# Rotation tables times the norm factor, level exponents by sign of scale, and a gating norm folded past its product

## The chip, the cores and the metric

The kernel runs on one core of a Trainium2 chip. The metric is device time in microseconds (us), the median of three runs. The core has TensorE (PE, matrix products, with its weight loads as PEld), VectorE (DVE), ScalarE (ACT) and GpSimd (POOL), and the queue of SyncE (SP), which here only issues DMA transfers. TensorE's clock has two levels, 1.2 and 2.4 GHz; the granted clock in the tables is its mean share of the upper one.

## The reference

A token matrix x of 512 by 1024 goes through two layers of a first block and one layer of a second block, all in float32.

- **First block, per layer.** h = rmsnorm(x) and one wide projection h @ w_in, whose columns feed three mixers. The *NSA mixer* has rotary positions on its queries and keys, a compressed branch over pooled key blocks, and two causal softmax branches, each weighted by a gate. The *GLA mixer* is a gated linear attention over chunks of 64 tokens; with b the running sum of log gates, pair (i, j) of a chunk is weighted by exp((b_i - b_j)/16). *Spatial gating* takes gelu(uv), splits it into u and v, puts v through a layernorm with gain g and bias b, mixes its tokens within chunks of 128 by a lower triangular matrix per group, adds a bias, and multiplies by u. The three results are concatenated, projected by w_out and added to x; a SwiGLU feed-forward layer follows.
- **Second block.** A gated linear recurrence in both directions beside a neighbourhood attention, two merge gates, an output projection w_o that is scaled and added to x1 = rmsnorm(x) * final_norm, and a last rmsnorm.

## The kernel before

Activations lie as eight tiles of 128 features by 512 tokens. Each float32 operand of a large product is split into a high and a low part, and each product is three matmuls of 512 columns (`three`). A weight chunk of 128 x 1024 comes by a DMA from the SP queue into `raw`; ScalarE rounds it to `whi` (L90, in `halves`) and `wlo` = raw - whi is one subtraction (L93). `turn` decides which engine does that subtraction: from L369, at the start of a layer's mixers, to L887, at their end, every second one goes to GpSimd, and otherwise all go to VectorE.

The mixers of a layer are nine generators, and the string WEAVE gives the order in which their steps are issued (WEAVE2 does the same in the second block). A scheduler then orders the instructions of each engine by its own time model; every engine runs its list in order and waits on semaphores. All tiles of 128 x 512 share 74 buffers (`slot`), and PSUM has eight banks.

The steps that matter here:

- `rotary`: a projection p is multiplied by the broadcast norm factor `rb` (L674, VectorE), and the result q1 is copied with its 32-row blocks exchanged into q2 by four DMAs from GpSimd's queue (L677). One projection later `finish` forms q1 times cosine (L648, VectorE), q2 times sine (L649, GpSimd) and their sum (L650, VectorE), and splits it into a query or a key (L659 and L660, or L663 to L667).
- `level` of `gla`: six levels per layer. GpSimd subtracts a reference column from each half of the running sum b with opposite signs (L465, L466), ScalarE takes one exponential (L467), and VectorE multiplies by k and q (L470, L471). The small products of 32 x 32 (`gram`) read the result.
- `gating`: the normalised v is multiplied by a gain and increased by a bias on GpSimd (L707, L708) before it enters the token mixing product.
- `compressed`: the softmax rows are scaled by a broadcast factor on GpSimd (L759).
- In the second block GpSimd multiplies x by its norm factor `rb1` (L1197), ScalarE multiplies by the gain (L1198) and the result is stored to HBM in `xdram` (L1199). It is loaded again before the last projection (L1224).

Of the kernel before, what the change touches and what calls it, by code (L numbers as in the profile page):

```python
# [16 lines left out]
P = 128  # L17
# [20 lines left out]
def body(tc, a, out):  # L38
# [37 lines left out]
        return slice(t * P, (t + 1) * P)  # L76


    turn = [0, 0]

    def fetch(src, n):
        raw = wraw.tile([P, 1024], F32, tag="raw", name="raw")
        dma(raw[:, :n], src)
# [2 lines left out]
    def halves(raw, nk, width):  # L86

        n = nk * width
        hi = whl.tile([P, 1024], F32R, tag="whi", name="whi")
        A.activation(hi[:, :n], raw[:, :n], AF.Copy)  # L90
        lo = whl.tile([P, 1024], F32R, tag="wlo", name="wlo")
        turn[0] += 1
        (G if turn[1] and turn[0] % turn[1] == 0 else V).tensor_tensor(lo[:, :n], raw[:, :n], hi[:, :n].bitcast(F32), op=ALU.subtract)  # L93
        return (hi[:, :n].rearrange("p (k c) -> p k c", c=width),
                lo[:, :n].rearrange("p (k c) -> p k c", c=width))

# [237 lines left out]
    for l in range(LAYERS):  # L334
# [31 lines left out]
        first = gemm(wi[6], act, lambda: stat.append(rsqrt(tok_stat(acc, D)[:], NT)))  # L366
        rs = stat[0]
        rb = bcast(rs)
        turn[1] = 2  # L369
        dma(gw[:16, :128], a["gla_w_up"][l])  # L370
        dma(gw[:, 128:132], a["gla_cols"][l])
        sv = [slot(shape=(P, 2, 256)) for _ in range(2)]
# [33 lines left out]
        def gla():  # L406
# [52 lines left out]
            def level(s_):  # L459
                n = S // (2 * s_)  # L460
                bb = b.rearrange("p (n h s) -> p n h s", h=2, s=s_)
                ref = bb[:, :, 0, s_ - 1:s_].to_broadcast([P, n, s_])
                X = slot()
                Xv = X.rearrange("p (n h s) -> p n h s", h=2, s=s_)
                G.tensor_tensor(Xv[:, :, 0], ref, bb[:, :, 0], op=ALU.subtract)  # L465
                G.tensor_tensor(Xv[:, :, 1], bb[:, :, 1], ref, op=ALU.subtract)  # L466
                A.activation(X[:], X[:], AF.Exp, scale=1.0 / 16)  # L467
                qv = q_.rearrange("p (n h s) -> p n h s", h=2, s=s_)
                kv = k_.rearrange("p (n h s) -> p n h s", h=2, s=s_)
                V.tensor_tensor(Xv[:, :, 0], Xv[:, :, 0], kv[:, :, 0], op=ALU.mult)  # L470
                V.tensor_tensor(Xv[:, :, 1], Xv[:, :, 1], qv[:, :, 1], op=ALU.mult)  # L471
                return X
# [169 lines left out]
        def rotary():  # L642
            for e in range(2):
                dma(trig[e][:], a["c_trig"][:, e])
            dma(amask[:], a["c_amask"])
            def finish(i, q1, q2):
                qr = slot()
                V.tensor_tensor(qr[:], q1[:], trig[0][:], op=ALU.mult)  # L648
                G.tensor_tensor(q2[:], q2[:], trig[1][:], op=ALU.mult)  # L649
                V.tensor_tensor(qr[:], qr[:], q2[:], op=ALU.add)  # L650
                if i < 4:
                    qn[i] = qr
                for g in range(2):
                    o = half[1 - g]
                    s_ = half[g]
                    t_ = slot(F32R)
                    if i < 4:
                        qs[4 * g + i] = t_
                        A.activation(t_[s_], qr[s_], AF.Copy, scale=0.125)  # L659
                        V.scalar_tensor_tensor(t_[o], qr[s_], 0.125, t_[s_].bitcast(F32), op0=ALU.mult, op1=ALU.subtract)  # L660
                    else:
                        kd[2 * (i - 4) + g] = t_
                        A.activation(t_[s_], qr[s_], AF.Copy)  # L663
                        A.activation(t_[o], qr[s_], AF.Copy)
                        l_ = slot(F32R)
                        G.memset(l_[o].bitcast(F32), 0.0)
                        V.tensor_tensor(l_[s_], qr[s_], t_[s_].bitcast(F32), op=ALU.subtract)  # L667
                        kl[2 * (i - 4) + g] = l_

            prev = None  # L670
            for i in (4, 5, 0, 1, 2, 3):
                p = proj(i)
                q1 = slot()
                V.tensor_tensor(q1[:], p[:], rb[:], op=ALU.mult)  # L674
                q2 = slot()
                for b_ in range(4):
                    dmag(q2[32 * b_:32 * b_ + 32], q1[32 * (b_ ^ 1):32 * (b_ ^ 1) + 32])  # L677
                if prev:
                    finish(*prev)
                prev = (i, q1, q2)  # L680
                yield
            finish(*prev)
            yield


        def gating():
            gb2 = slot(shape=(P, 2, 256))
            dma(gb2[:], a["sg_gb"][l].partition_broadcast(P))
            wT = slot(shape=(P, 4, P))
            dma(wT[:], a["sg_wT"][l])  # L690
            G.affine_select(wT[:], wT[:], pattern=[[0, 4], [1, P]], compare_op=ALU.is_ge, fill=0.0, base=0, channel_multiplier=-1)
            for g in range(4):
                dma(bs[half[g % 2], g // 2], a["sg_b"][l, g].partition_broadcast(64))
            mv = small.tile([P, NT, 2], F32, tag="sgmv", name="sgmv")
            for th in range(2):
                gelu2(sv[th].rearrange("p a b -> p (a b)"), sv[th].rearrange("p a b -> p (a b)"), S, slot(), slot())
# [7 lines left out]
            for t in range(NT):  # L704
                vg = sv[t // 2][:, t % 2]
                V.tensor_scalar(vg, vg, mv[:, t, 0:1], rl[:, t:t + 1], op0=ALU.subtract, op1=ALU.mult)
                G.tensor_tensor(vg, vg, gb2[:, 0], op=ALU.mult)  # L707
                G.tensor_tensor(vg, vg, gb2[:, 1], op=ALU.add)  # L708
            us = []
            for gp_ in range(2):  # L710
                p = proj(12 + gp_)
# [5 lines left out]
            for gp_ in range(2):  # L717
                u = us[gp_]
                p = bank()
                for t in range(NT):  # L720
                    for par in range(2):
                        g = 2 * gp_ + par
                        mm(p[half[par], tsl(t)], sv[t // 2][:, t % 2, 64 * g:64 * g + 64], wT[:, g])
                s1 = slot()
                V.tensor_tensor(s1.rearrange("p (t i) -> p t i", t=NT), p.rearrange("p (t i) -> p t i", t=NT),
                                bs[:, gp_, None, :].to_broadcast([P, NT, P]), op=ALU.add)
                V.tensor_tensor(s1[:], s1[:], u[:], op=ALU.mult)
                split(s1[:], osg[gp_][0][:], osg[gp_][1][:], 0.5)
            yield
# [4 lines left out]
        def compressed():  # L734
            dma(cm[:], a["c_cmask"])
            pcs = []
            for ih in range(2):
# [18 lines left out]
                for i in range(2):  # L756
                    sv_ = sm.rearrange("p (q i g) -> p q i g", q=NT, i=2)[:, :, i]
                    V.tensor_tensor(sv_, sv_, gate[:, :, 6 * ih + 3 * i::12], op=ALU.mult)
                G.tensor_tensor(pcf, pcf, sm[:, :, None].to_broadcast([P, 16, 32]), op=ALU.mult)  # L759
                pcs.append(pc)  # L760
            yield
            for ih in range(2):
# [121 lines left out]
            for _ in t:  # L884
                pass

        turn[1] = 0  # L887

        heads = ogla + osg + onsa
        x = [slot() for _ in range(KT)]  # L890
# [301 lines left out]
    for n, c in enumerate(WEAVE2):  # L1192
# [1 line left out]
        if n == 0:  # L1194
            rb1 = bcast(rsqrt(tok_stat(acc, D)[:], NT))
        if n < KT:
            G.tensor_tensor(x[n][:], x[n][:], rb1[:], op=ALU.mult)  # L1197
            A.activation(x[n][:], x[n][:], AF.Copy, scale=norms[:, 4, n:n + 1])  # L1198
            dma(xdram[:, n], x[n][:])  # L1199
    for c in "rpn":  # L1200
        for _ in tasks[c]:
# [20 lines left out]
    xo = [slot() for _ in range(KT)]  # L1222
    for j in range(KT):
        dma(xo[j][:], xdram[:, j])  # L1224
    for j in range(KT - 1):
        p = gemm(a["w_o"][j], mg)
        V.scalar_tensor_tensor(xo[j][:], p[:], mod[:, 2, j:j + 1], xo[j][:], op0=ALU.mult, op1=ALU.add)
# [89 lines left out]
def _prep(inp):  # L1317
# [32 lines left out]
    gn = np.concatenate([inp["gla_norm"]] * 2, 1)  # L1350
    z = np.zeros_like(gn)
    r["gla_cols"] = np.ascontiguousarray(np.stack([inp["gla_b_up"], gn, z, z], 2))
    r["sg_gb"] = np.stack([inp["sg_ln_g"], inp["sg_ln_b"]], 1)
    r["sg_wT"] = np.ascontiguousarray(inp["sg_w"].transpose(0, 3, 1, 2))
    r["sg_b"] = inp["sg_b"]
    rows = np.concatenate([np.concatenate([np.arange(64 * i, 64 * i + 64), np.arange(64 * (i + 4), 64 * (i + 4) + 64)])
# [57 lines left out]
```

## Time and profile before

| | |
|---|---|
| median of 3 runs | 1908.09 us (1907.3 to 1911.67) |
| the profiled execution | 1909.09 us, span 1907.4 us |
| mean granted TensorE clock | 0.986 |
| busy, share of the span | PE 97%, DVE 58%, ACT 43%, POOL 15% |
| first layer's mixers | about 30 to 251 us |
| second layer's mixers | about 690 to 907 us |
| second block | about 1319 us to the end |

A stretch is read from the span's start. Busy time of TensorE counts pipelined matmuls, which overlap, so a busy TensorE is not yet one at full rate: a 512-column matmul follows the one before after about 0.22 us at the upper clock level and after about 0.43 us at the lower. A wait names the instruction that released the waiting one.

### The profile page before, as it was taken

How to read it: one execution, taken by the hardware profiler on the slowest of the kernel's cores; microseconds unless marked ns; L12 is line 12 of the kernel's file. 1: busy time of each engine (PE TensorE's matmuls, PEld its weight loads, DVE VectorE, ACT ScalarE, POOL GpSimd, SP SyncE). 2: the span in 40 equal slices, each digit the busy share in tenths (PEclk: the TensorE clock that was granted, in tenths of full speed). 3: DMA queues.
4: the chain of work that ended last, by engine and by line, in shares of the span. 5: the costliest groups of instructions: out<-in, count | busy, mean ns of one | idle time of the engine just before them, and what ended most of it. 6: DMA issues, size and time to landing. Idle time of an engine off the chain costs nothing.

```text
span 1907.4 us, 27296 instructions
## 1 busy us (share of the span) xinstructions
PE 1853.2 (97%) x10770; PEld 1510.4 (79%) x10770; DVE 1100.0 (58%) x2043; ACT 822.8 (43%) x1406; POOL 280.9 (15%) x346
## 2 busy tenths in 40 slices
PE   8899999999999998999999999999989999999997
PEld 7677678888888886876788888888778878888886
DVE  5778754756642346978445555324568867664333
ACT  6345732323222233456323322223477857662223
POOL 3643011000000035620200000011600030000003
PEclk9999999999999998999999999999999999999998
DMA  8421032544533372310332332332433342322331
GB/s 249 147 79 56 1 107 90 186 144 132 166 109 117 106 235 64 99 34 1 131 96 93 100 100 90 98 93 84 138 116 97 103 135 88 100 89 89 99 133 67
DMA packets 71441, 203.22 MB, mean 107 GB/s; under 512 B 11632, under 2 KB 15120, under 8 KB 71312
## 3 DMA queue, kind: packets, MB, share of 16 engines
q1 hardware_dynamic: 66768, 192.03, 31.5%
q0 software_dynamic: 4544, 9.44, 2.0%
q8 instruction: 84, 1.38, 0.3%
q14 instruction: 45, 0.37, 0.1%
HBM read 186.23 MB, written 6.29 MB: 101 GB/s over the span
## 4 chain that ended last, share of the span: by engine, by line
PE 91%; DVE 4%; ACT 2%; issue 1%; DMA 1%; POOL 0%; SPq 0%; POOLq 0%; DVEq 0%; ACTq 0%
PE bank L45 88%; PE bank L806 2%; PE bank L1122 1%; ACT whi L90 1%; DVE wlo L93 1%; DVE b L789 0%; DVE b L660 0%; DMA raw<-w_in_m 0%; DVE b L470 0%; DVE b L648 0%; ACT b L267 0%; ACT b L1037 0%; DMA raw<-w_gate 0%; DMA c<-c 0%; ACT b L1105 0%
## 5 line engine op out<-in xcount | busy, mean ns | idle before, releaser
L45 PE MATMUL bank<-b,whi 128*128 128x512 f32 (+1 forms) x4220 | 1299.5, 390 | 0.0
L45 PEld LDWEIGHTS bank<-b,whi 128*128 128x128 f32 x4220 | 788.9, 189 | 164.8 <-issue 5.1
L45 PE MATMUL bank<-b,wlo 128*128 128x512 f32 (+1 forms) x2110 | 818.7, 388 | 0.2 <-DVE wlo L93 0.2
L90 ACT ACTIVATE whi<-raw 128x1024 fp32r<-128x1024 f32 (+2 forms) x290 | 298.8, 1032 | 713.4 <-PE bank L45 465.0
L93 DVE TENSOR_TENSOR wlo<-raw,whi 128x1024 fp32r<-128x1024 f32 (+3 forms) x273 | 330.4, 1211 | 296.6 <-ACT whi L90 291.7
L45 PEld LDWEIGHTS bank<-b,wlo 128*128 128x128 f32 x2110 | 398.6, 189 | 83.6 <-issue 1.6
L45 PE MATMUL bank<-b 32*32 32x32 f32 (+9 forms) x2956 | 201.0, 260 | 18.5 <-DVE b L471 8.2
L217 POOL TENSOR_TENSOR b<-b 128x512 f32<-128x512 f32 x33 | 50.8, 1546 | 1001.4 <-ACT b L211 1001.2
L45 PEld LDWEIGHTS bank<-b 32*32 32x32 f32 (+3 forms) x2956 | 134.1, 128 | 71.0 <-issue 49.0
L45 PE MATMUL bank<-whi,b 128*128 128x512 f32 (+1 forms) x384 | 111.5, 370 | 6.8 <-ACT b L267 6.8
L272 ACT ACTIVATE b<-b 128x512 fp32r<-128x512 f32 x76 | 48.0, 632 | 136.5 <-DVE b L926 92.2
L792 ACT ACTIVATE b<-b,nm 128x384 f32<-128x384 f32 (+3 forms) x128 | 71.0, 559 | 34.6 <-DVE nm L789 34.2
L45 PEld LDWEIGHTS bank<-whi,b 128*128 128x128 f32 x384 | 71.3, 195 | 16.9 <-ACT b L267 6.8
L789 DVE CUSTOM_DVE_ANT_0 b<-bank,b 128x384 f32<-128x384 f32 (+3 forms) x128 | 56.8, 485 | 26.5 <-PE bank L45 26.5
L45 PE MATMUL bank<-wlo,b 128*128 128x512 f32 (+1 forms) x192 | 70.2, 368 | 0.0
L924 DVE TENSOR_TENSOR b<-bank,b 128x512 f32<-128x512 f32 x44 | 30.3, 689 | 65.1 <-PE bank L45 65.1
L922 DVE TENSOR_TENSOR b<-bank,b 128x512 f32<-128x512 f32 x44 | 30.3, 688 | 52.7 <-PE bank L45 51.9
L274 DVE TENSOR_TENSOR b<-b 128x512 fp32r<-128x512 f32 x72 | 49.7, 691 | 18.6 <-ACT b L272 18.6
L324 DVE SCALAR_TENSOR_TENSOR b<-raw,silc,b 128x512 f32<-128x512 f32 x42 | 29.6, 747 | 36.6 <-DMA raw<-w_c 36.6
L806 PEld LDWEIGHTS bank<-c_ident,b 128*128 128x128 f32 x320 | 35.5, 141 | 18.8 <-DVE b L796 5.7
L806 PE MATMUL bank<-c_ident,b 128*128 128x128 f32 x320 | 46.8, 278 | 3.7 <-DVE b L796 3.7
L93 POOL TENSOR_TENSOR wlo<-raw,whi 128x1024 fp32r<-128x1024 f32 x17 | 41.3, 2427 | 51.7 <-ACT whi L90 49.9
(254 smaller groups left out, 1511.6 us busy)
## 6 DMA issues: line engine op xcount, KB each, us to landing
raw<-w_in SPq DMA_DIRECT2D x56, 512.0 KB, 3.5
raw<-w_gate SPq DMA_DIRECT2D x44, 512.0 KB, 3.5
raw<-w_up SPq DMA_DIRECT2D x44, 512.0 KB, 3.5
raw<-w_down SPq DMA_DIRECT2D x32, 512.0 KB, 3.5
raw<-w_in_t SPq DMA_DIRECT2D x28, 512.0 KB, 3.8
raw<-w_c SPq DMA_DIRECT2D x24, 512.0 KB, 3.5
b<-cmp_w SPq DMA_DIRECT2D x32, 256.0 KB, 7.4
raw<-w_out SPq DMA_DIRECT2D x16, 512.0 KB, 3.5
```

Source lines behind the costliest of these rows:

```text
L45: T.matmul(o, l, r, start=st, stop=sp)
L90: A.activation(hi[:, :n], raw[:, :n], AF.Copy)
L93: (G if turn[1] and turn[0] % turn[1] == 0 else V).tensor_tensor(lo[:, :n], raw[:, :n], hi[:, :n].bitcast(F32), op=ALU.subtract)
L217: self.eng.tensor_tensor(self.acc[:], self.acc[:], self.last[:], op=ALU.add)
L272: A.activation(hi, src, AF.Copy, scale=scale)
L274: V.tensor_tensor(lo, src, hi.bitcast(F32), op=ALU.subtract)
L324: V.scalar_tensor_tensor(ma[e][:], r_, sc_[:, k:k + 1], ma[e][:], op0=ALU.mult, op1=ALU.add)
L789: V.tensor_tensor_reduce(out=pg[qb], in0=p, in1=amask[:, S - w:], op0=ALU.add, op1=ALU.min, scale=-1.0, scalar=-NEG, accum_out=nm[:, qb:qb ...
L792: A.activation(pg[qb], pg[qb], AF.Exp, bias=nm[:, qb:qb + 1], scale=-1.0, accum_out=dn[:, qb:qb + 1])
L806: T.transpose(p[:, c0 + (qb - kb) * P:c0 + (qb - kb + 1) * P], ph[g][qb][:, tsl(kb)], ident[:])
L922: V.tensor_tensor(g1[:], pg[:], rb[:], op=ALU.mult)
L924: V.tensor_tensor(u1[:], pu[:], rb[:], op=ALU.mult)
```

## The change

It takes the two-input elementwise operations of 128 x 256 and larger off GpSimd in the mixers and in the second block's start, and changes some of the arithmetic around them. All splits of weights go to VectorE. A level becomes one subtraction b - ref over the whole tile on VectorE, and two exponentials on half tiles with scales -1/16 and +1/16. The cosine and sine tables are multiplied by `rb` once per layer on VectorE; the projection is copied to q1 by ScalarE unscaled, the cosine product reads the projection's bank, and the sine product moves to VectorE. The gating gain is applied behind the token mixing product, and its bias is folded into the additive term through the column sums of the triangular matrix (four small products with a vector of ones per layer, two small VectorE operations). The spill of x is stored as it is, and norm factor and gain are applied on VectorE after it is loaded again; `rb1` is kept until then. GpSimd keeps its memsets, copies, DMA issues, the triangular select, the small powers, and the sums of squares (L217).

```diff
     def halves(raw, nk, width):
...
-        turn[0] += 1
-        (G if turn[1] and turn[0] % turn[1] == 0 else V).tensor_tensor(lo[:, :n], raw[:, :n], hi[:, :n].bitcast(F32), op=ALU.subtract)
+        V.tensor_tensor(lo[:, :n], raw[:, :n], hi[:, :n].bitcast(F32), op=ALU.subtract)
...
             def level(s_):
...
-                ref = bb[:, :, 0, s_ - 1:s_].to_broadcast([P, n, s_])
+                ref = bb[:, :, 0, s_ - 1:s_].to_broadcast([P, n, 2 * s_])
...
-                G.tensor_tensor(Xv[:, :, 0], ref, bb[:, :, 0], op=ALU.subtract)
-                G.tensor_tensor(Xv[:, :, 1], bb[:, :, 1], ref, op=ALU.subtract)
-                A.activation(X[:], X[:], AF.Exp, scale=1.0 / 16)
+                V.tensor_tensor(X.rearrange("p (n m) -> p n m", m=2 * s_), b.rearrange("p (n m) -> p n m", m=2 * s_), ref, op=ALU.subtract)
+                for e in range(2):
+                    A.activation(Xv[:, :, e], Xv[:, :, e], AF.Exp, scale=(2 * e - 1) / 16.0)
...
-            def finish(i, q1, q2):
-                qr = slot()
-                V.tensor_tensor(qr[:], q1[:], trig[0][:], op=ALU.mult)
-                G.tensor_tensor(q2[:], q2[:], trig[1][:], op=ALU.mult)
+            for e in range(2):
+                V.tensor_tensor(trig[e][:], trig[e][:], rb[:], op=ALU.mult)
+
+            def finish(i, qr, q2):
+                V.tensor_tensor(q2[:], q2[:], trig[1][:], op=ALU.mult)
                 V.tensor_tensor(qr[:], qr[:], q2[:], op=ALU.add)
...
-                V.tensor_tensor(q1[:], p[:], rb[:], op=ALU.mult)
+                A.activation(q1[:], p[:], AF.Copy)
+                qr = slot()
+                V.tensor_tensor(qr[:], p[:], trig[0][:], op=ALU.mult)
...
         def gating():
-            gb2 = slot(shape=(P, 2, 256))
-            dma(gb2[:], a["sg_gb"][l].partition_broadcast(P))
+            gb2 = wtile([P, 4], "sggb", pl=lp)
+            dma(gb2[:], a["sg_cols"][l])
...
+            p = bank()
+            for g in range(4):
+                mm(p[half[g % 2], tsl(g // 2)], ones[:].to_broadcast([P, 64]), wT[:, g])
+            for gp_ in range(2):
+                V.scalar_tensor_tensor(bs[:, gp_], p[:, tsl(gp_)], gb2[:, 2 + gp_:3 + gp_], bs[:, gp_], op0=ALU.mult, op1=ALU.add)
...
-                G.tensor_tensor(vg, vg, gb2[:, 0], op=ALU.mult)
-                G.tensor_tensor(vg, vg, gb2[:, 1], op=ALU.add)
...
-                V.tensor_tensor(s1.rearrange("p (t i) -> p t i", t=NT), p.rearrange("p (t i) -> p t i", t=NT),
-                                bs[:, gp_, None, :].to_broadcast([P, NT, P]), op=ALU.add)
+                V.scalar_tensor_tensor(s1.rearrange("p (t i) -> p t i", t=NT), p.rearrange("p (t i) -> p t i", t=NT),
+                                       gb2[:, gp_:gp_ + 1], bs[:, gp_, None, :].to_broadcast([P, NT, P]), op0=ALU.mult, op1=ALU.add)
...
-                G.tensor_tensor(pcf, pcf, sm[:, :, None].to_broadcast([P, 16, 32]), op=ALU.mult)
+                V.tensor_tensor(pcf, pcf, sm[:, :, None].to_broadcast([P, 16, 32]), op=ALU.mult)
...
         if n < KT:
-            G.tensor_tensor(x[n][:], x[n][:], rb1[:], op=ALU.mult)
-            A.activation(x[n][:], x[n][:], AF.Copy, scale=norms[:, 4, n:n + 1])
             dma(xdram[:, n], x[n][:])
...
         dma(xo[j][:], xdram[:, j])
+        V.scalar_tensor_tensor(xo[j][:], xo[j][:], norms[:, 4, j:j + 1], rb1[:], op0=ALU.mult, op1=ALU.mult)
```

## Rows read from the trace of the kernel before

**Rows 1.** The page's first part: engine, busy time (share of the span), instructions.

```profile
PE 1853.2 (97%) x10770; PEld 1510.4 (79%) x10770; DVE 1100.0 (58%) x2043; ACT 822.8 (43%) x1406; POOL 280.9 (15%) x346
```

**Rows 2.** A stretch: its length, each engine's busy time (instructions), granted clock, DMA share, GB/s.

```profile
30.00:251.00 221.00, 209.22 (x1961) 158.39 (x1962) 165.65 (x433) 114.65 (x265) 77.28 (x99) 0.96 0.28 83
```

**Rows 3.** TensorE's waits in three stretches (30:251, 690:907, 1319:1400): total, times, longest.

```profile
PE bank L45 <- DVE b L660: 3.6, 1, 3.6
PE bank L45 <- DVE b L471: 3.4, 1, 3.4
...
PE bank L45 <- DVE b L471: 4.8, 2, 4.2
...
PE bank L45 <- DVE b L660: 1.3, 1, 1.3
...
PE bank L1122 <- DVE b L1110: 6.4, 1, 6.4
PE bank L45 <- ACT b L1162: 1.5, 1, 1.5
```

**Rows 4.** Timeline of VectorE: start, duration, line, operation, tiles, shapes, count.

```profile
63.95 3.19 DVE L667 TENSOR_TENSOR b<-b 64x512 fp32r<-64x512 f32 x1
...
69.31 4.93 DVE L93 TENSOR_TENSOR wlo<-raw,whi 128x1024 fp32r<-128x1024 f32 x1
...
87.82 6.59 DVE L660 SCALAR_TENSOR_TENSOR b<-b 64x512 fp32r<-64x512 f32 x2 [0.28 <-ACT b L659]
...
719.66 1.22 DVE L93 TENSOR_TENSOR wlo<-raw,whi 128x1024 fp32r<-128x1024 f32 x1
...
725.99 2.59 DVE L648 TENSOR_TENSOR b<-b 128x512 f32<-128x512 f32 x1
728.50 4.13 DVE L470 TENSOR_TENSOR b<-b 128x256 f32<-128x256 f32 x1
```

**Rows 5.** Timeline of GpSimd at the same times; columns as in rows 4.

```profile
69.57 0.60 POOL L465 TENSOR_TENSOR b<-b 128x256 f32<-128x256 f32 x1
...
727.98 2.00 POOL L677 DMA_DIRECT2D b<-b  x4
729.99 2.35 POOL L93 TENSOR_TENSOR wlo<-raw,whi 128x1024 fp32r<-128x1024 f32 x1
```

**Rows 6.** Stretches around TensorE's stalls; columns as in rows 2.

```profile
75.10:80.40 5.30, 5.30 (x74) 4.37 (x75) 2.31 (x5) 4.47 (x12) 3.20 (x6) 0.50 0.47 127
...
93.90:97.80 3.90, 3.90 (x13) 3.23 (x14) 3.25 (x14) 1.77 (x6) 0.00 (x0) 0.57 0.02 4
...
733.20:739.70 6.50, 6.50 (x77) 5.33 (x78) 4.99 (x5) 3.79 (x9) 2.73 (x4) 0.51 0.28 83
...
751.00:756.60 5.60, 5.60 (x16) 4.54 (x17) 3.83 (x15) 2.66 (x8) 0.00 (x0) 0.50 0.01 3
...
1368.30:1374.00 5.70, 5.70 (x26) 4.78 (x27) 4.71 (x5) 1.41 (x2) 5.59 (x6) 1.00 0.34 109
...
...
1392.10:1396.00 3.90, 3.90 (x16) 3.45 (x17) 2.46 (x10) 3.87 (x6) 0.00 (x0) 0.64 0.45 172
```

**Rows 7.** The chain of waits from 1369.9 to 1400.1 us: shares by line.

```profile
by line: PE bank L45 49.5%; PE bank L1122 9.4%; ACT b L1198 8.2%; ACT whi L90 6.7%; ACT b L1105 6.0%; ACT b L1037 5.8%; DVE wlo L93 4.1%; ACT b L1004 3.2%; ACT b L1040 2.3%; DVE b L1043 2.0%; DVE dn L1107 1.6%; DVE b L1110 1.1%; issue 0.6%;
```

**Rows 8.** Groups by line, whole span: count, busy, mean ns of one, idle before.

```profile
L93 POOL TENSOR_TENSOR wlo<-raw,whi 128x1024 fp32r<-128x1024 f32 x17 | 41.3, 2427 | 51.7 <-ACT whi L90 49.9 <-DMA b<-cmp_w 1.6
...
L649 POOL TENSOR_TENSOR b<-b 128x512 f32<-128x512 f32 x12 | 16.9, 1410 | 12.3 <-DMA b<-b 7.7 <-DMA b<-c_trig 4.6
...
L467 ACT ACTIVATE b<-b 128x512 f32<-128x512 f32 x12 | 7.4, 624 | 3.3 <-POOL b L466 3.2
...
L727 DVE TENSOR_TENSOR b<-b 128x512 f32<-128x512 f32 x4 | 2.8, 689 | 0.1
```

**Rows 9.** The rotary exchange's DMA issues (ns min/median/max) and their landing.

```profile
L677 POOL DMA_DIRECT2D b<-b x48: 496/496/603, 47.8 to 777.3; - x48
...
DMA to landing us min/median/max: 1.8/2.4/6.4
```

More of the change, by code (lines that the diff above doesn't have):

```diff
@@ L76, in tsl @@
         return slice(t * P, (t + 1) * P)
-    turn = [0, 0]
     def fetch(src, n):
@@ L368, in body @@
         rb = bcast(rs)
-        turn[1] = 2
         dma(gw[:16, :128], a["gla_w_up"][l])
@@ L679, in rotary @@
                     finish(*prev)
-                prev = (i, q1, q2)
+                prev = (i, qr, q2)
                 yield
@@ L885, in body @@
                 pass
-        turn[1] = 0
         heads = ogla + osg + onsa
@@ L1352, in _prep @@
     r["gla_cols"] = np.ascontiguousarray(np.stack([inp["gla_b_up"], gn, z, z], 2))
-    r["sg_gb"] = np.stack([inp["sg_ln_g"], inp["sg_ln_b"]], 1)
+    r["sg_cols"] = np.stack([np.concatenate([_cols(inp["sg_ln_g"][l]), _cols(inp["sg_ln_b"][l])], 1) for l in range(LAYERS)])
     r["sg_wT"] = np.ascontiguousarray(inp["sg_w"].transpose(0, 3, 1, 2))
```

## Prediction

> **What bounds the kernel now.** I read the page's engines first: TensorE is busy for 97% of the span, VectorE 58%, GpSimd 15% [rows 1]. An engine so full can gain only from its own idle time and from slow clock, so the removed GpSimd work is worth nothing by its busy time. Second, the stretches: in the first layer's mixers TensorE is busy 209.22 of 221 us at a clock of 0.96, and VectorE 165.65 [rows 2]. Third, TensorE's waits there. They are few and nearly all name VectorE: 3.6 and 3.4 us in the first layer (for L660 and L471), 4.8 and 1.3 us in the second, and 6.4 us at the start of the second block [rows 3].
>
> Fourth, the timeline at these waits. Ahead of the 3.4 us wait VectorE's weight split took 4.93 us, where the same split takes 1.22 at another place; while it ran, GpSimd worked through a string of two-input operations, the first of them at 69.57 [rows 4, 5]. The pair L660 took 6.59 us, and L648 and L470 in the second layer 2.59 and 4.13, L470 while GpSimd's own split ran [rows 4, 5]. A 512-column two-input operation takes 0.69 elsewhere [rows 8]. So the operations that TensorE waits for are stretched beside GpSimd.
>
> Fifth, the clock. Behind three of these stalls TensorE works at 0.50 to 0.57 for 5.3, 3.9 and 6.5 us, the lower of its two levels; behind the 1.5 us wait for L1162, which ended just before 1368.3, it stays at 1.00 [rows 3, 6]. A stall thus costs more than its length.
>
> **The mixers.** I call the stalls A (3.4 us) and B (3.6) in the first layer, C (4.2, the longest of the 4.8) and D (the other 0.6 and 1.3) in the second [rows 3].
>
> A: VectorE is late by 4.93 - 1.22 = 3.7 for the split and by 3.19 - 0.69 = 2.5 for L667, together 6.2 [rows 4, 8]. It takes over, in the same stretch, one split (1.22), two level subtractions and a rotary product (0.69 each): 3.3. The net, 2.9 of 3.4 us, comes back.
> B: the pair is late by 6.59 - 1.38 = 5.2. The same 3.3 us of new work may stand ahead of it or behind. Ahead, 1.9 comes back, behind, the whole 3.6; I take 2.6.
> C: L648 is late by 1.9 and L470 by at least 3.4 (4.13 against 0.69 for a tile twice as wide), 5.3 in all; two subtractions and a product (2.1) come in. I take 3.3.
> D: the lateness is smaller and the new work is as large; 0.
> Idle time: 2.9 + 2.6 + 3.3 = 8.8 us.
>
> The clock behind A, B and C costs 5.3 x 0.50 + 3.9 x 0.43 + 6.5 x 0.49 = 7.5 us [rows 6]. What remains of these stalls is under the 1.5 us behind which the clock held, so I take 6, not all, because the products of 32 x 32 follow there too. Mixers: 14.8.
>
> The rows can be weighed against a rule. The Trainium skill, page "SBUF — State Buffer", section "SBUF: two separate sides", says that GpSimd shares a pair of ports with VectorE's operations that read two SBUF tensors, and that whichever starts first holds the pair for one whole instruction. By that bound the split at 69.31 loses 0.60 us, the length of L465, and not the 3.7 that the trace shows; A would give nothing, B and C about 2 each, and with the clock behind A the time would be some 8 us above mine, 1899, where the second rival below ends. Here the measurement differs from the page: the delay lasts over several GpSimd instructions in a row, so the rule gets no chance beyond that rival's.
>
> **What the rest costs.** VectorE gains 17 splits x 1.22 + 12 levels x 0.69 + 12 rotary products x 0.69 + 4 table products + 4 of L759 (0.69 each) + 4 small bias operations (at most 0.69 each) = 46 us in both mixers at most. The lateness in rows 4 alone is 16.5 of it, so VectorE's net load rises by up to 30 us over two stretches in the first of which it is idle for 55 [rows 2, 4, 8]. That idle time hides it; where it stands ahead of an operation that TensorE waits for, it costs its full length. That is a rival below.
>
> ScalarE: a half-tile exponential costs between half of 624 ns and all of it, so twelve levels cost 0 to 7.5 us more, and six copies per layer of about that length are added [rows 8]. ScalarE is busy 114.65 of 221 us and none of the mixer stalls names it [rows 2, 3]: 0, with 7.5 kept as the upper end.
>
> TensorE: eight more small products. In the nearest row 26 matmuls of 512 columns took 5.70 us, 0.22 each [rows 6]: at most 1.8, at least 0 if they fall into idle time; I take 1.0. They wait for the triangular select, and behind them on TensorE stand the projections of the weave; the select follows a DMA that is issued at the same point as before.
>
> The four DMAs per rotary exchange now follow a ScalarE copy in place of a VectorE product of equal length, and on GpSimd's queue they are no longer behind splits and subtractions: 0, gain left out. The broadcast load of gain and bias becomes a small one: 0.
>
> **The second block's start.** The chain of waits through the 6.4 us wait runs over ScalarE for a third of its length, and 8.2% of its 30.2 us, 2.5 us, are the gain product L1198 [rows 3, 7]; it is removed. The clock of 0.64 over the next 3.9 us costs 1.4; half of it comes back, 0.7. The eight spills no longer wait for GpSimd and ScalarE, so on the SP queue the weight loads issued behind them come earlier; I count nothing for it. Sum 3.2.
>
> After the reload VectorE has eight products of about 0.69, 5.5 us, over the last projection, whose eight sums it makes one per product of 24 matmuls (24 x 0.22 = 5.3 us): hidden. Uncovered it would be 5.5. `rb1` keeps one of 74 buffers through the second block, while the eight of x come free earlier: 0, at most one stall like A, 3.4.
>
> **Sum.** 14.8 + 3.2 - 1.0 = 17.0 us. The profiled execution, 1909.09 (span 1907.4 and 1.7 around it), becomes 1892.1; it stands 1.0 above the median, so the median 1908.1 becomes 1891.1.
>
> **The rivals.**
>
> *All of it comes back.* Stalls A to D and the second block's are 3.6 + 3.4 + 4.8 + 1.3 + 6.4 = 19.5 us, and the slow clock behind them 7.5 + 2.8 + 1.4 = 11.7 [rows 3, 6]. Time: 1908.1 - 31.2 = 1877. For it: the scheduler's order no longer rests on durations that GpSimd stretches. Against it: VectorE's new work. Chance 0.15.
>
> *GpSimd's remaining work blocks too.* L470 started at 728.50, within four DMA issues, a while before GpSimd's split began at 729.99 [rows 4, 5]. If issues and memsets block as well, half of the mixers' 14.8 goes: 1898. Against it: the split of 1.22 us at 719.66 ran beside the same four issues. Chance 0.10.
>
> *VectorE takes over.* If its new work stands ahead of what TensorE waits for everywhere, the 14.8 goes and 3.2 - 1.0 remain: 1906. For it: it is already busy for 75% of the first mixer. Chance 0.14.
>
> *VectorE stands still at the exchange; slower.* The sine product waits for the exchanged rows. Before, GpSimd bore that wait, 7.7 us in all [rows 8]; now VectorE does, and weight splits and level products queue behind it for which TensorE waits. A landing takes 1.8 to 6.4 us, median 2.4 [rows 9]. If each of the twelve costs TensorE 2.4, that is 28.8, and 1891 becomes 1920; it decides from 17.0 / 12 = 1.4 us each. Against it: a projection of 5.3 us lies between issue and use, and GpSimd waited little. Chance 0.11. The Trainium skill, same page and section, warns that descriptors of GpSimd-issued DMAs starve while VectorE holds the shared pair in a two-port mode, which would make the exchange later still. The 48 issues took 496 to 603 ns beside a busy VectorE [rows 9], which shows no such starving.
>
> **How the numbers follow.** My forecast, 1891, has a chance of 0.50, with 1883 to 1899 as its own range. The low end of the range is the first rival's with 1 us below it, 1876; upward it reaches past *VectorE takes over* to 1908, which leaves out the exchange and little else, under 0.2. 0.2% (3.8 us) is about what a measurement of this kernel can tell from no change. Faster by more: 0.50 + 0.15 + 0.10 + a part of the 0.14 (0.03) = 0.78; within: 0.10; slower: 0.12, the exchange and a remnant of *VectorE takes over*.
>
> **What would show it.** Right: L667, L93, L660, L648 and L470 all near 0.69 or 1.22 us in the mixers; TensorE's waits for L471 and L660 gone or under 1.5 us each; a granted clock above 0.98 in both mixers; the wait for L1110 near 4; TensorE's busy time a few us lower, from the clock. Wrong: waits of VectorE on the exchange DMAs of over 1.4 us; VectorE's idle time gone just ahead of the level products; a new wait on ScalarE's exponentials; stretched VectorE operations beside memsets or DMA issues.

## The result and the profile after

The changed kernel took 1885.91 us (median of 4 runs, 1883.0 to 1891.64) against 1908.15 us (1907.3 to 1911.67): a ratio of 0.9884, 95% interval 0.9857 to 0.991. The forecast was 1891 with a range of 1876 to 1908. The profiled execution took 1886.07 us, its span is 1884.4, and its mean granted clock is 0.993.

The page's first part, as in [rows 1]. TensorE's busy time fell by 8.4 us and VectorE's by 9.9, although VectorE has 49 instructions more; GpSimd's fell by 106.3.

```profile
PE 1844.8 (98%) x10786; PEld 1504.2 (80%) x10786; DVE 1090.1 (58%) x2092; ACT 823.0 (44%) x1420; POOL 174.6 (9%) x265
```

To say where the 23.0 us of the two spans lie, I cut both traces at the same points of the work: the first matmul of w_out in each layer, the start of the second layer's mixers, and the end of the second block's first part. These are stretches of the kernel before: length, busy time (instructions) of PE, PEld, DVE, ACT and POOL, granted clock, DMA share, GB/s.

```profile
30.00:251.02 221.02, 209.24 (x1961) 158.41 (x1962) 165.67 (x433) 114.67 (x265) 77.28 (x99) 0.96 0.28 83
693.08:906.94 213.86, 204.94 (x1936) 154.91 (x1935) 167.23 (x426) 110.74 (x257) 77.36 (x98) 0.96 0.25 74
1323.35:1399.69 76.34, 66.99 (x308) 55.80 (x309) 47.82 (x102) 44.30 (x75) 32.26 (x47) 0.93 0.42 128
```

And these are the stretches of the changed kernel between the same points:

```profile
30.00:242.43 212.43, 206.69 (x1969) 156.46 (x1970) 160.25 (x452) 117.13 (x276) 33.63 (x63) 0.98 0.28 85
684.39:887.51 203.12, 198.91 (x1943) 150.68 (x1943) 158.11 (x445) 114.11 (x269) 32.95 (x61) 1.00 0.26 76
1303.92:1378.07 74.15, 67.13 (x304) 55.77 (x305) 46.48 (x106) 38.10 (x68) 20.14 (x39) 0.93 0.36 107
```

The mixers are 8.6 and 10.7 us shorter, the second block's start 2.2. Of the mixers' 19.3 us, 10.8 are idle time of TensorE (11.8 + 8.9 before, 5.7 + 4.2 after), and 8.6 are busy time, which goes with the clock: 0.96 in both mixers before, 0.98 and 1.00 after. VectorE is busy for 5.4 and 9.1 us less, with more to do.

The changed kernel's VectorE groups (line, operation, tiles, shapes, count, busy, mean ns, idle before). The first row is from the first layer's mixers alone (30 to 243 us), the others are from the whole span. L90 is the weight split (L93 before), L657 and L664 the splits of a key and a query (L660, L667), L646 and L647 the sine product and the sum, L461 the new level subtraction, L466 and L467 the level products (L470, L471).

```profile
L90 DVE TENSOR_TENSOR wlo<-raw,whi 128x1024 fp32r<-128x1024 f32 x18 | 22.0, 1220 | 6.2 <-ACT whi L88 6.1
...
L657 DVE SCALAR_TENSOR_TENSOR b<-b 64x512 fp32r<-64x512 f32 x16 | 11.0, 686 | 0.5
...
L647 DVE TENSOR_TENSOR b<-b 128x512 f32<-128x512 f32 x12 | 8.2, 687 | 0.2
L646 DVE TENSOR_TENSOR b<-b 128x512 f32<-128x512 f32 x12 | 8.2, 686 | 5.0 <-DMA b<-b 5.0
...
L461 DVE TENSOR_TENSOR b<-b 128x512 f32<-128x512 f32 x12 | 7.8, 681 | 0.0
...
L664 DVE TENSOR_TENSOR b<-b 64x512 fp32r<-64x512 f32 x8 | 5.5, 682 | 0.1
...
L466 DVE TENSOR_TENSOR b<-b 128x256 f32<-128x256 f32 x12 | 5.1, 422 | 0.2
L467 DVE TENSOR_TENSOR b<-b 128x256 f32<-128x256 f32 x12 | 5.0, 418 | 0.0
```

Every one is at the time of an undisturbed operation (1.22, 0.69 and 0.42 us); the split at the place of stall A (71.14 us in this trace) takes 1.22 us where it took 4.93 [rows 4]. The exchange's wait has moved to VectorE, 5.0 us in all.

TensorE's waits in the first layer's mixers (30 to 243 us), in the second layer's (684 to 888), and around the second block's start (1300 to 1378), one block after another:

```profile
PE bank L45 <- issue: 2.6, 1, 2.6
PE bank L809 <- DVE b L799: 1.8, 1, 1.8
PE bank L45 <- POOL rs L245: 1.2, 1, 1.2
PE bank L45 <- DVE b L429: 1.0, 1, 1.0
...
PE bank L809 <- DVE b L799: 1.8, 1, 1.8
PE bank L45 <- issue: 1.7, 2, 0.9
PE bank L45 <- POOL b L690: 0.5, 1, 0.5
...
PE bank L1124 <- DVE b L1112: 4.8, 1, 4.8
...
```

The waits on level products and key splits of [rows 3] are gone altogether. Largest in the first block's mixers is now a wait of 2.6 us in which TensorE waited for nothing that the profile shows (the kernel before has one of 1.6 us at that place), and the second block's wait is 4.8 us in place of 6.4.

### The profile page after: what moved, and what is told of

The parts are those of the page before. It is cut to its first block, busy times and chain, and to the rows that moved or that the text cites. A ratio compares the mean times of both kernels' runs of the same rounds, so it can differ in the third digit from the quotient of the medians.

```text
span 1884.4 us, 27302 instructions
## 1 busy us (share of the span) xinstructions
PE 1844.8 (98%) x10786; PEld 1504.2 (80%) x10786; DVE 1090.1 (58%) x2092; ACT 823.0 (44%) x1420; POOL 174.6 (9%) x265
## 4 chain that ended last, share of the span: by engine, by line
PE 93%; DMA 2%; DVE 2%; ACT 1%; issue 1%; SPq 0%; POOL 0%; POOLq 0%; DVEq 0%; ACTq 0%
PE bank L45 91%; PE bank L809 2%; PE bank L1124 1%; DMA b<-cmp_w 1%; DMA b<-c_trig 1%; ACT whi L88 0%; DMA raw<-w_in_m 0%; DVE b L792 0%; DVE wlo L90 0%; ACT b L264 0%; DMA raw<-w_gate 0%; DVE b L728 0%; DVE b L730 0%; POOL b L1259 0%; DVE grb L550 0%
## 5 line engine op out<-in xcount | busy, mean ns | idle before, releaser
L88 ACT ACTIVATE whi<-raw 128x1024 fp32r<-128x1024 f32 (+2 forms) x290 | 298.8, 1032 | 714.5 <-PE bank L45 471.3
L90 DVE TENSOR_TENSOR wlo<-raw,whi 128x1024 fp32r<-128x1024 f32 (+2 forms) x290 | 346.2, 1195 | 302.0 <-ACT whi L88 296.9
L799 DVE TENSOR_SCALAR b<-b,dn 128x512 f32<-128x512 f32 (+3 forms) x128 | 40.7, 382 | 0.7
```

Of the source, the lines that this page charges most:

```text
L90: V.tensor_tensor(lo[:, :n], raw[:, :n], hi[:, :n].bitcast(F32), op=ALU.subtract)
L799: V.tensor_scalar(pg[qb], pg[qb], dn[:, qb:qb + 1], None, op0=ALU.mult)
```

## The experiments

Two theories stood against each other. **Shared access:** a GpSimd operation that reads SBUF holds up VectorE's, so TensorE waits and its clock drops behind the wait. **Late results:** GpSimd is slow and stood in the chain, and moving or rewriting its steps shortened the chain. A third possibility was that the rewritten arithmetic, or the new order that the scheduler made of it, earned the time. Experiments that share a chip share the runs of the kernel before.

**1. The second block's part alone** (the kernel before, with only this).

```diff
-            G.tensor_tensor(x[n][:], x[n][:], rb1[:], op=ALU.mult)
-            A.activation(x[n][:], x[n][:], AF.Copy, scale=norms[:, 4, n:n + 1])
...
+        V.scalar_tensor_tensor(xo[j][:], xo[j][:], norms[:, 4, j:j + 1], rb1[:], op0=ALU.mult, op1=ALU.mult)
```

> Kernel before with the second block's part of the change alone (x stored unscaled, norm factor and gain applied after the reload). The two traces put 2.2 us between the end of the second mixers and the first attention output of the second block and 1.6 us on the rest. If the parts simply add, this run is 2 to 4 us faster than before (about 1905). If the mixers' gain owes something to this part (buffers freed, another order), it is more than 6 us faster; if the new order of the whole kernel is what counts, it may as well be slower.

Measured: 1906.06 us against 1908.37, ratio 0.9987 (0.9972 to 1.0002). TensorE still waits 8.1 us for L471 and 5.1 for L660; its wait for L1110 is 4.8 us as in the full change. So this part is worth about 2.3 us, with an interval that just includes no gain, and the mixers' time comes from elsewhere.

**2. The engine alone.** The kernel before with the mixers' two-input GpSimd operations given to VectorE one for one, and no arithmetic rewritten: the level is still two subtractions and one exponential, rotary and gating are as before.

```diff
-                G.tensor_tensor(Xv[:, :, 0], ref, bb[:, :, 0], op=ALU.subtract)
-                G.tensor_tensor(Xv[:, :, 1], bb[:, :, 1], ref, op=ALU.subtract)
+                V.tensor_tensor(Xv[:, :, 0], ref, bb[:, :, 0], op=ALU.subtract)
+                V.tensor_tensor(Xv[:, :, 1], bb[:, :, 1], ref, op=ALU.subtract)
...
-                G.tensor_tensor(q2[:], q2[:], trig[1][:], op=ALU.mult)
+                V.tensor_tensor(q2[:], q2[:], trig[1][:], op=ALU.mult)
```

(and likewise the weight splits, the gain and bias of the gating, and L759)

> Kernel before with only the engine of the mixers' two-input GpSimd operations changed to VectorE (splits, both level subtractions, sine product, gain and bias of the gating, scaling of the compressed softmax); no table scaling, no exponents by sign, no folded norm, old spill. Theory of the shared access: the presence of two-input operations on GpSimd stretches VectorE, so nearly all of the mixers' 19 us comes back, 1889 to 1894, although VectorE then has about 8 us more work than in the changed kernel. Rival, the rewritten arithmetic (shorter chains, fewer VectorE operations) is what pays: less than half, 1899 or more.

Measured: 1889.12 us (1888.25 to 1890.81), ratio 0.99 (0.9886 to 0.9913): 19.3 us of the 22. VectorE's busy time is 1100.9 us, as before the change, though it has 73 instructions more. That is the plainest sign of the stretch: the moved work filled the time that the stretching had used up. It doesn't part the two theories yet, since late results would be cured by the same move.

**3. Every second weight split back on GpSimd** (the changed kernel, with `turn` as before).

> Changed kernel with every second weight split of the mixers on GpSimd again (17 operations, none of them on a chain by itself, since three buffers lie between split and product). Theory of the shared access: GpSimd's splits, the longest of its operations at 2.4 us, again stretch VectorE's two-input operations: 4 to 10 us slower than the changed kernel (1890 to 1896), with VectorE operations of 2 to 3 us in the trace. Rival, GpSimd's slowness on the chains was what cost: no change, since the splits are not on a chain.

Measured: 1891.24 us (1889.11 to 1894.2), ratio 0.9911 (0.9897 to 0.9925). The key split takes 846 ns on the mean in place of 686 (the longest 3.25 us), the rotary sum 1032 in place of 687 (the longest 2.77), and TensorE waits 1.9 us for a level product again.

**4. Level subtraction and sine product back on GpSimd.**

```diff
-                V.tensor_tensor(X.rearrange("p (n m) -> p n m", m=2 * s_), b.rearrange("p (n m) -> p n m", m=2 * s_), ref, op=ALU.subtract)
+                G.tensor_tensor(X.rearrange("p (n m) -> p n m", m=2 * s_), b.rearrange("p (n m) -> p n m", m=2 * s_), ref, op=ALU.subtract)
...
-                V.tensor_tensor(q2[:], q2[:], trig[1][:], op=ALU.mult)
+                G.tensor_tensor(q2[:], q2[:], trig[1][:], op=ALU.mult)
```

> Changed kernel with the level subtraction (one operation over the whole tile) and the sine product on GpSimd again, 24 operations of 1.3 us. Theory of the shared access: VectorE operations stretched, 4 to 10 us slower than the changed kernel. Rival, slowness on the chain: each is 0.6 us longer than on VectorE and at most a few of the 24 are on TensorE's path, so 1 to 4 us slower, with VectorE's durations unchanged.

Measured: 1892.43 us (1888.42 to 1894.86), ratio 0.9916 (0.9902 to 0.9929). The key split takes 941 ns, the sum 1000, L467 583; TensorE waits 3.8 us for L467. Here VectorE also waited 4.3 us for GpSimd's sine product, so both theories have a hand in it. By the ratios, experiments 3 and 4 each give back some 5 or 6 us of the 22; the interval of each overlaps that of the changed kernel (0.9857 to 0.991).

**5 and 6. GpSimd work that nobody reads.** The changed kernel with subtractions on GpSimd whose result nothing uses, after every second weight split, every level and every rotary sum; and the same with one-input copies, two for each subtraction.

```diff
+            G.tensor_tensor(dead[:, :384], hi[:, 0:384].bitcast(F32), lo[:, 0:384].bitcast(F32), op=ALU.subtract)
...
+                G.tensor_tensor(dead[:, :256], X[:, 0:256], b[:, 0:256], op=ALU.subtract)
...
+                G.tensor_tensor(dead[:, :256], qr[:, 0:256], trig[0][:, 0:256], op=ALU.subtract)
```

> Changed kernel with dead work added in the mixers: two-input subtractions on GpSimd whose result nobody reads, over tiles that the level products, the rotary sums and every second weight split have just made (102 operations of 256 or 384 columns, as much data as the removed operations had). Theory of the shared access: though nothing waits for them, VectorE's two-input operations are stretched to 2 us and more and the time goes back by 8 to 20 us (1894 to 1906). Rivals, GpSimd's slowness on the chain or the rewritten arithmetic: no change within 3 us.

> The same dead work on GpSimd as copies with one input (two copies in place of each subtraction, same data read). If any GpSimd instruction that reads SBUF stretches VectorE, it is as slow as with the two-input dead work, 8 to 20 us above the changed kernel. If it takes two inputs, it is within 3 us of the changed kernel.

Measured: 1907.37 us (ratio 0.9997, 0.9985 to 1.0008) with the subtractions, 1926.49 us (1.0095, 1.0078 to 1.0113) with the copies. Neither is a clean answer. TensorE's largest wait with the subtractions, and then with the copies:

```profile
PE bank L45 <- POOL b L703: 12.6, 2, 8.4
```

```profile
PE bank L45 <- ACT whi L90: 26.6, 5, 11.3
```

L703 is the triangular select of the gating, queued on GpSimd behind the dead work, and the column sums of the changed kernel need it early. In the second, the dead copies read the weight buffers, and ScalarE waited 16.6 us for them before it could fill the next. VectorE was stretched in both (the key split 906 and 754 ns), but the price is that of a queue and of a buffer. The failure is mine: dead work has to lie where nothing waits for its queue or for its inputs.

**7. The same dead subtractions on VectorE.**

> The same dead subtractions on VectorE: 24 pairs of 256 columns at about 0.42 us each, and some 17 splits in three pieces of about 0.5, 0.5 and 0.42 us, together 44 us more VectorE work in the mixers. It tells what VectorE's load costs by itself. If the idle time of VectorE hides it, less than 4 us; if VectorE is next to bound (it is busy for about 73% of both mixers), 10 us or more, and then the change has paid its gain net of such a cost.

Measured: 1891.44 us (1889.8 to 1892.47), ratio 0.991 (0.9894 to 0.9925). VectorE's busy time is 39.5 us above the changed kernel's, its durations stay undisturbed (L646's and L647's counterparts 688 ns, the level products 420), and the time is some 5 us longer, between the two outcomes that I had named. So a large load on VectorE costs something in these stretches, but far less than its own length.

**8. The disputed cost by itself.** This kernel leaves out the whole computation. It sets twelve VectorE operations of 128 x 512 beside ten or sixteen GpSimd instructions, phase after phase, kind against kind.

> It leaves out the whole computation and only sets twelve VectorE operations of 128 x 512 beside ten to sixteen GpSimd instructions, kind against kind, each phase behind a common start. Solo, a VectorE addition of two SBUF tiles takes 0.69 us. Shared access: beside GpSimd additions it takes 1.2 us or more each, and GpSimd's own grow as well over their solo length; beside memsets and DMA issues it stays within 5% of 0.69; with one input in PSUM, or as a copy, it stays near its solo time. Rival (GpSimd was only late, not in the way): all VectorE durations within 5% of solo in every phase, and the stretched ones of the kernel come from something else. What one-input GpSimd copies do is open: 0.69 if only two-input operations collide, near 1.0 if every GpSimd read of SBUF does.

VectorE's timeline (start, duration of the group, line, operation, shapes, count): two-input additions alone; beside GpSimd additions; beside GpSimd copies; beside memsets; beside DMA issues; additions with one input in PSUM beside GpSimd additions; copies alone; copies beside GpSimd additions.

```profile
7.98 8.69 DVE L69 TENSOR_TENSOR v<-p,q 128x512 f32<-128x512 f32 x12 [7.98 <-ACT v L94]
33.64 17.79 DVE L69 TENSOR_TENSOR v<-p,q 128x512 f32<-128x512 f32 x12 [16.98 <-ACT v L94]
67.51 11.85 DVE L69 TENSOR_TENSOR v<-p,q 128x512 f32<-128x512 f32 x12 [16.07 <-ACT v L94]
95.40 8.68 DVE L69 TENSOR_TENSOR v<-p,q 128x512 f32<-128x512 f32 x12 [16.04 <-ACT v L94]
107.45 8.68 DVE L69 TENSOR_TENSOR v<-p,q 128x512 f32<-128x512 f32 x12 [3.37 <-ACT v L94]
142.99 8.67 DVE L71 TENSOR_TENSOR v<-pz,q 128x512 f32<-128x512 f32 x12 [26.86 <-ACT v L94]
158.26 5.51 DVE L73 COPY v<-p 128x512 f32<-128x512 f32 x12 [6.61 <-ACT v L94]
164.46 14.90 DVE L73 COPY v<-p 128x512 f32<-128x512 f32 x12 [0.69 <-ACT p L88]
```

GpSimd's timeline of the same kernel: additions alone; beside VectorE's additions; copies alone; beside VectorE's additions; additions beside VectorE's with a PSUM input; additions beside VectorE's copies.

```profile
17.93 13.32 POOL L77 TENSOR_TENSOR g<-r,s 128x512 f32<-128x512 f32 x10 [17.48 <-ACT r L90]
33.17 16.27 POOL L77 TENSOR_TENSOR g<-r,s 128x512 f32<-128x512 f32 x10 [1.92 <-ACT g L93]
54.38 10.73 POOL L79 COPY g<-r 128x512 f32<-128x512 f32 x16 [4.95 <-ACT g L93]
67.02 14.84 POOL L79 COPY g<-r 128x512 f32<-128x512 f32 x16 [1.90 <-ACT g L93]
...
142.52 13.34 POOL L77 TENSOR_TENSOR g<-r,s 128x512 f32<-128x512 f32 x10 [3.31 <-ACT g L93]
165.02 14.05 POOL L77 TENSOR_TENSOR g<-r,s 128x512 f32<-128x512 f32 x10 [9.16 <-ACT r L90]
```

Shared access is there without any queue, buffer or result in common: twelve additions take 17.79 us in place of 8.69, and GpSimd's ten 16.27 in place of 13.32. GpSimd copies disturb too, 11.85. Memsets and DMA issues don't (8.68), nor does a GpSimd addition disturb a VectorE addition that takes one input from PSUM (8.67). One expectation missed: VectorE's copies did not stay near their time alone but took 14.90 us for 5.51.

**9 to 11. On one chip: the changed kernel again, both engine moves without rewritten arithmetic, and dead work at a harmless place.** Number 10 is the kernel before with the edits of experiments 1 and 2. Number 11 adds to number 10 two subtractions of 128 x 256 behind each level and each rotary sum, 48 in all, whose result nothing reads; no weight buffer is held, and TensorE needs no early select here.

```diff
+                for e in range(2):
+                    G.tensor_tensor(dead[:], X[:, 256 * e:256 * e + 256], b[:, 256 * e:256 * e + 256], op=ALU.subtract)
...
+                for e in range(2):
+                    G.tensor_tensor(dead[:], qr[:, 256 * e:256 * e + 256], trig[0][:, 256 * e:256 * e + 256], op=ALU.subtract)
```

> The changed kernel once more, for a ratio on the same chip as the kernels beside it: 1884 to 1890, ratio 0.987 to 0.991. Both theories expect the same.

> The two-input operations of the mixers on VectorE and the second block's part, but the arithmetic of levels, rotary and gating as before. If the engine is what matters: 19 us from the mixers' engine and 2 from the spill, together 1886 to 1889, within 3 us of the changed kernel. Rival, the rewritten arithmetic carries the gain: 1895 or more.

> The kernel with both engine moves, with 48 GpSimd subtractions of two 128 x 256 tiles added behind the levels and the rotary sums, whose result nothing reads and which hold no buffer that TensorE's operands need. Shared access: VectorE's operations beside them are stretched, TensorE waits again for the level products or splits, 4 to 10 us over the kernel without them. Rival (GpSimd matters only where its result or its queue is waited for): within 2 us of the kernel without them, no TensorE wait on a level product.

Measured: the changed kernel 1886.74 us (1884.87 to 1888.64), ratio 0.9887 (0.9868 to 0.9907); the engine moves alone 1882.66 (1881.4 to 1888.56), 0.9873 (0.9851 to 0.9895); with the dead work 1895.38 (1893.18 to 1904.29), 0.9937 (0.9915 to 0.996). Number 10 can't be told from the full change: the rewritten arithmetic earns nothing that these runs show. The dead work costs 12.7 us, more than I expected. Its VectorE groups (L665 is the key split, L652 the sine product, L653 the sum, L467 and L472 a level's second subtraction and second product):

```profile
L665 DVE SCALAR_TENSOR_TENSOR b<-b 64x512 fp32r<-64x512 f32 x16 | 11.8, 740 | 0.5
L652 DVE TENSOR_TENSOR b<-b 128x512 f32<-128x512 f32 x12 | 11.2, 930 | 0.2
L653 DVE TENSOR_TENSOR b<-b 128x512 f32<-128x512 f32 x12 | 11.1, 926 | 0.1
...
L467 DVE TENSOR_TENSOR b<-b 128x256 f32<-128x256 f32 x12 | 8.2, 685 | 0.0
...
L472 DVE TENSOR_TENSOR b<-b 128x256 f32<-128x256 f32 x12 | 7.1, 595 | 0.0
```

And TensorE's largest wait in that kernel:

```profile
PE bank L45 <- DVE b L665: 8.4, 2, 4.4
```

In number 10 this split takes 687 ns and TensorE waits 0.5 us for it. The dead results are read by no one, so "late results" can't explain it: 42 us of GpSimd reading brought back two stalls of 4.4 and 4.1 us, and the granted clock fell from 0.992 to 0.989. VectorE's timeline in number 11 ahead of the first stall (L672 is the split of a query):

```profile
74.71 2.73 DVE L672 TENSOR_TENSOR b<-b 64x512 fp32r<-64x512 f32 x2
...
85.36 0.94 DVE L467 TENSOR_TENSOR b<-b 128x256 f32<-128x256 f32 x1
...
87.00 1.40 DVE L665 SCALAR_TENSOR_TENSOR b<-b 64x512 fp32r<-64x512 f32 x2
```

In number 10 VectorE does the same operations in the same order from 70.28 us to the split at 83.01, with 2.8 us of waiting among them. In number 11, from 71.95 to 87.00, they take 5.0 us longer in all and VectorE never waits; the split itself takes its usual time. So neither a new order nor a wait for GpSimd made TensorE's stall, but the stretched operations ahead of the split.

**12. The changed kernel without the fold of the gating norm** (gain and bias ahead of the product, on VectorE; no column sums).

> The changed kernel with the gating gain and bias applied ahead of the token mixing product again, but on VectorE: eight small products per run and four small VectorE operations fewer, sixteen VectorE operations of 128 x 256 more (about 0.42 us each, 6.7 us of VectorE time). If the fold costs what the prediction took for it (1.0 us of TensorE) and VectorE's extra work is hidden: 1882 to 1887, up to 4 us under the changed kernel. Rival, the fold carries a part of the gain because VectorE's two operations per tile hold up the token mixing product: 1889 or more.

Measured: 1885.01 us (1883.52 to 1886.62), ratio 0.9876 (0.9859 to 0.9892). No difference from the changed kernel that can be measured.

## Why the prediction was right, and by how much it was off

**The mechanism held.** GpSimd's operations stretched VectorE's, TensorE stalled behind these, and its clock stayed low behind the stalls. Experiment 2 shows that the engine alone accounts for the mixers, 8 that the stretch exists without any dependence, 11 that it costs TensorE time. The trace of before already had it. These are GpSimd's rows beside the stretched L667 (63.95 us, 3.19) and the stretched split (69.31, 4.93) of [rows 4]:

```profile
64.17 2.40 POOL L93 TENSOR_TENSOR wlo<-raw,whi 128x1024 fp32r<-128x1024 f32 x1
...
70.14 0.62 POOL L466 TENSOR_TENSOR b<-b 128x256 f32<-128x256 f32 x1
70.73 0.61 POOL L465 TENSOR_TENSOR b<-b 128x256 f32<-128x256 f32 x1
71.30 0.64 POOL L466 TENSOR_TENSOR b<-b 128x256 f32<-128x256 f32 x1
71.90 1.26 POOL L649 TENSOR_TENSOR b<-b 128x512 f32<-128x512 f32 x1
```

L667's own 0.69 and GpSimd's 2.40 are 3.09 of its 3.19. The split's own 1.22 and the string of five from 69.57 [rows 5] to 73.16, 3.59, are 4.81 of its 4.93: it stood still while GpSimd read without a pause. One row doesn't add up: L470 at 728.50 [rows 4] has 0.42 of its own and 2.35 beside GpSimd's split, together 2.77 of its 4.13. The rest lies beside four DMA issues [rows 5], which disturb nothing in experiment 8; it stays open.

Late results have little part in these stalls. In the mixers of before VectorE waited for a result of GpSimd three times (1.2, 1.9 and 2.5 us, at 128, 177 and 832 us), never ahead of a stall. ScalarE waited for the level subtraction twice, just ahead of A and B:

```profile
70.80 0.63 ACT L467 ACTIVATE b<-b 128x512 f32<-128x512 f32 x1 [1.81 <-POOL b L466]
...
90.82 0.63 ACT L467 ACTIVATE b<-b 128x512 f32<-128x512 f32 x1 [1.38 <-POOL b L466]
```

Both exponentials were done about 3 us before VectorE came to the end of the stretched split (74.24) and of the stretched pair L660 (94.41). What late results cost elsewhere in the mixers was not measured by itself; experiment 4 has both.

**The mixers were sized too small: 19.3 us where the sum had 13.8** (14.8 less 1.0). Three steps contribute:

- *Idle time, 8.8 forecast, 10.8 measured.* I charged VectorE's new operations against A, B and C and gave D nothing. All four stalls, 13.1 us, vanished, and other waits took 2.3 of it. The charge held an error: the rotary product is no new work, since the product with `rb` leaves VectorE for it (the 49 added instructions are 17 splits, 12 subtractions, 4 table products, 4 of L759, 4 for the bias and 8 after the reload). The new work is thus at most 37 us and not 46, and with 0.69 less at each stall the same reckoning gives 3.4 (the whole of A), 3.1 and 3.9, together 10.4. (The lateness in [rows 4] sums to 16.7, not 16.5; nothing hangs on it.) The operations that are new cost VectorE nothing on balance, since the operations around them shrank by more: its busy time in the mixers fell by 14.5 us. My netting counted only the stretched operations in [rows 4]; many more were stretched (L471 took 665 ns on the mean and L667 1091, their counterparts above 418 and 682).
- *Clock, 6 forecast.* TensorE's busy time fell by 8.6, and it did so with the 16 small matmuls of the column sums added. I priced the stretches behind A, B and C alone, at 7.5, and took 6; the 5.6 us at 0.50 behind D [rows 6], 2.8 us, were in no term, because D was given nothing.
- *The added products, 1.0 forecast.* In the row below, eight of them took 0.66 us, so 1.3 in both layers. Experiment 12, without them, is not measurably different. The size was right.

**The second block's start: 3.2 forecast, 2.2 in its stretch.** The wait was foreseen near 4 and is 4.8. The clock there is 0.93 in both kernels, so the 0.7 for the clock did not come. A further 1.4 us lies later in the block, where TensorE waited for L1110 twice before (3.5 us) and now once (1.8), which experiment 1 shows as well.

**Covers.** The twelve added ScalarE exponentials cost 1.1 us of ScalarE (8.5 against 7.4 us) and no TensorE wait names them. The reload's eight products left no wait.

**The rivals.** *All of it comes back* (1877): the mixers' stalls did, but the second block's wait kept 4.8 of 6.4 us, and the wait of 1.6 us without a releaser grew to 2.6. *GpSimd's remaining work blocks too* (1898): memsets and DMA issues left twelve additions at 8.68 us, so they do not. GpSimd's copies, which also remain, do disturb in experiment 8 (11.85), but the groups of the changed kernel above don't show it. *VectorE takes over* (1906): 39.5 us more on VectorE cost about 5 us in experiment 7. *VectorE stands still at the exchange* (1920): it does, 5.0 us in all and 2.4 at most, where GpSimd had 7.7 [rows 8]. That is one of the signs of being wrong that I had named (over 1.4), yet no wait of TensorE's matmuls follows; the weight splits and level products behind it had that much room.

**The length of the hold.** L667 waited for one whole GpSimd instruction, the split for five in a row, though by the records both had begun first, by 0.22 and 0.26 us. In experiment 8 an addition on each side would take 0.69 + 1.33 = 2.02 us if neither ran while the other did; GpSimd's ten took 16.27 beside VectorE's, about 1.6 each, and two of VectorE's in the middle of them 3.30. The Trainium skill, page "SBUF — State Buffer", section "SBUF: two separate sides", says that a VectorE operation with two SBUF inputs collides with a GpSimd operation that reads SBUF, and one in a two-port mode with any, and that whichever starts first holds the ports for its whole instruction. Experiment 8 agrees on which additions collide (memsets 8.68 us, a PSUM operand 8.67); on the order and the length the traces differ from the page, five instructions in the one case and less than one in the other, and the measurement decides. What sets the length was not tried.

**What stays open.** The wait of 2.65 us. This is TensorE's timeline of the changed kernel around it:

```profile
123.89 1.24 PE L45 MATMUL bank<-b 32*32 32x32 f32 x114
127.78 0.32 PE L45 MATMUL bank<-b 32*32 32x32 f32 x14 [2.65 <-issue]
128.03 0.66 PE L45 MATMUL bank<-b,ones 128*64 128x128 f32 x8
...
129.41 1.03 PE L45 MATMUL bank<-b,whi 128*128 128x512 f32 x2
...
133.06 0.63 PE L45 MATMUL bank<-b,whi 128*128 128x512 f32 x2
```

It lies inside a run of 32 x 32 products, with nothing for TensorE to wait for, and behind it pairs of matmuls take 1.03 us, while from 133 us on they take 0.63; the granted clock is 0.79 from 125 to 133 us. Experiments 2, 10 and 12 have it as well (2.3 to 2.5 us), experiment 11 with 3.7, 5 and 7 with 0.7 and 0.8, the kernel before with 1.6. It therefore doesn't come from the rewritten arithmetic. One lead lies in the traces: in all of these kernels it comes after the same number of TensorE's records (weight loads, matmuls and semaphore waits in order of time), 2753, and the two shorter ones in the changed kernel's second mixers (0.9 us at 735.31, 0.76 at 768.37) come after 9665 and 10433, which is 27 and 30 times 256 further on. So it seems to go with the count of instructions and not with what they compute. What happens at such a count no run here shows.

## What to carry to other kernels

When an operation takes several times its usual length, look at what GpSimd reads at that moment before looking at the operation: an elementwise step put on GpSimd to relieve VectorE can cost VectorE more than it takes off. Before rewriting arithmetic, move the operations to the other engine one for one and measure that; here this alone gave 19.3 of the 22 us, and with the second block's part all of them. A test with dead work only tells something if neither its queue nor its inputs are needed by anyone else.

## What the runs showed of the hardware that was not expected

- Of the kinds tried, VectorE's one-input copies between SBUF tiles suffer most: twelve took 5.51 us alone and 14.90 beside GpSimd additions, which themselves lost little (14.05 against 13.32).
- One-input GpSimd copies, which the expectation left open, disturb VectorE as well: twelve additions took 11.85 us, and sixteen copies 14.84 in place of 10.73.
- One operand in PSUM took an addition out of the collision on both sides: 8.67 us for VectorE's twelve, as expected, and 13.34 for GpSimd's ten, against 13.32 alone.
